# One layer of a hybrid decoder on one Trainium2 core: transposes given out inside the next product, query projections moved ahead

## The chip, the core and the metric

The kernel runs on one core of a Trainium2 chip. Six things work side by side on it: PE (the matrix engine, which also transposes by a product with the identity), DVE (the vector engine), ACT (the scalar engine, with tables for exponential, tanh and the like), POOL (the general engine), SP (here it only gives out transfers), and the DMA engines that carry them. Each engine takes its own instructions strictly in order and waits by semaphore for what another has to deliver. The metric is the device time of the whole program in microseconds (us); less is better.

## What is computed

One layer for 256 tokens of width 2048, in float32 accuracy, cut to what matters here:

```python
h = rmsnorm(x, pre_mix_norm)
z = h @ w_in                          # 2*1024 conv columns, 768 q latent, 512 kv latent, 64 rotary key
u = a * sigmoid(g)                    # GLU on the conv columns
u = silu(layernorm(causal_depthwise_conv(u, conv_w, conv_b)))     # 31 taps, over 1024 channels
q = rmsnorm(q_lat) @ w_uq             # 8 heads: 128 plain columns and 64 rotary ones each
kv = rmsnorm(kv_lat) @ w_ukv          # 8 heads: 128 key and 128 value columns each
q_pe, k_pe = apply_rope(q_pe), apply_rope(k_rope)      # one rotary key for all heads
attn = causal_attention(concat(q_nope, q_pe), concat(k_nope, k_pe), v)
mix = concat(rmsnorm(u), rmsnorm(attn)) @ w_out
x = x + rmsnorm(mix)
hf = rmsnorm(x)
x = x + rmsnorm((silu(hf @ w_gate) * (hf @ w_up)) @ w_down)       # inner width 5632
```

## The kernel before

**Products.** Every large product is made of three products of half-precision parts: a weight block is brought into a float32 stage buffer (four of them), ACT makes its high part (`whi`, L97) and DVE the rest (`wlo`, L98), in blocks of up to 2048 columns by 128 rows. For each row tile of a weight and each of the two token blocks of 128, PE then does high times high (L142), high times low (L143) and low times high (L144), for 512 columns at a time as a rule; two accumulators `acc` take the two token blocks. `mm3` is that loop; `mm3t` (L151 to L153) is the same the other way round, for 128 columns by 256 tokens, in an accumulator `tmp`.

**Stages.** (1) Four column blocks of the conv group. After each, ACT makes tanh and a scaled copy `av`, DVE makes `u` (L302), PE transposes it (L305) and ACT copies the result to `upad`. (2) Three blocks of 448 latent columns; ACT copies them out (L348), `latent_norm` scales the query latent and the kv latent (L330), splits them, and sends both through a transposing DMA. (3) The shared rotary key `kp`: eight small DVE operations a token block, the last L370, then a PE transpose L371; the rotary queries: one product of 36 matmuls, a copy `zq` (L381), six DVE operations a token block (L387 to L392), four transposes (L395). (4) The values, 48 matmuls. (5) Eight heads: `project` makes queries and keys of a head, two heads ahead; `scores` multiplies them (L447, L448), DVE takes the maximum (L453), ACT the exponential, POOL scales by the sum (L467); `attend` transposes the probabilities (L472 to L474), multiplies by the values, and POOL adds the squares (L486). (6) The attention rows of the output projection, four column blocks; between them the layer norm of the conv output: `ln_mean` (sum over channels L515, its mean over partitions L517, sum of squares after subtracting it L520), `ln_var` (L525, L531), swish, `conv_norm` (sums L538, L543). (7) The conv rows, then the feed-forward part, gate and up and down, which holds most of the products.

The depthwise convolution itself (31 taps for each of four channel groups, L275 and L283 on DVE, with some taps on ACT, L281) is given out in portions, `pump(n)`, between the other stages; the tuple `PUMPS` says how many taps after which.

**What sets the order.** The code is written in one sequence, and the scheduler that compiles it keeps an order for each engine that follows from that sequence and from a model of when inputs are there, so that a transposition written after a product may be placed some matmuls into the next. Transfers are all given out by SP's queue in one order; a stage buffer that is not free holds the queue behind it.

Of the kernel before, what the change touches and what calls it, by code (L numbers as in the profile page):

```python
# [17 lines left out]
P = 128  # L18
S = 256
# [22 lines left out]
# Exact power-of-two scales that centre the half-precision parts of an operand.  # L42
# [8 lines left out]
def hymba_layer(ctx: ExitStack, tc: tile.TileContext, x, xT, pos, inv_freq, g_pre, w_in, w_lat,  # L51
# [84 lines left out]
    def mm3(ps, x_of, wgt, tbs=(0, 1), k0=0, start=True, stop=True):  # L136
# [9 lines left out]
    def mm3t(ps, x_of, wgt, c0):  # L146
        """Feature-major product of 128 columns: ps += w[:, c0:c0+128].T @ x."""
# [43 lines left out]
    def rstd_of(ss, n, w=1, out_tile=None):  # L191
        """(ss / n + eps) ** -0.5"""
# [72 lines left out]
    def conv_tap(quarter, k):  # L265
        """One tap of a quarter of the channels, on the vector engine or shared with the scalar engine."""
# [22 lines left out]
    for j in range(4):  # L289
        if j == 0:  # L290
            ps = ps0
        else:
            wgt = wg1 if j == 1 else Weights(KD, 512).load(w_in[j], W_S)
            ps = [acc_tile(), acc_tile()]
            mm3(ps, h_of, wgt)
        for tb in range(NTB):
# [6 lines left out]
            tp = tmp_tile()  # L303
            for i in range(2):
                nc.tensor.transpose(tp[:, i * P : (i + 1) * P], u[:, i * P : (i + 1) * P], ident)  # L305
            nc.scalar.copy(upad[:, 2 * j : 2 * j + 2, PAD + tb * P : PAD + (tb + 1) * P],
                           tp[:, : 2 * P].rearrange("p (c t) -> p c t", c=2))
        conv_todo += [(j, k) for k in range(TAPS)]
        pump(PUMPS["conv"][j])

# [30 lines left out]
    # the columns are in the order query latent, kv latent, shared rotary key  # L341
    LN = (KL + QL + ROPE) // 3
    for j in range(3):
        wgt = Weights(KD, LN).load(w_lat[j], W_S)
        ps = [acc_tile()[:, :LN], acc_tile()[:, :LN]]
        mm3(ps, h_of, wgt)
# [10 lines left out]
    kpT = region(33, (S,))  # L357
    tp = tmp_tile()
    for tb in range(NTB):
        kp = work.tile([P, 2, ROPE], F32, tag="kp", name=nm("kp"))  # L360
        t1 = work.tile([P, ROPE], F32, tag="kt1", name=nm("kt1"))
        sin, cos = sincos[:, tb, 0, :], sincos[:, tb, 1, :]
        x1, x2 = z_kr[:, tb, 0:HALF], z_kr[:, tb, HALF:ROPE]
        nc.vector.tensor_tensor(t1[:, 0:HALF], x2, sin, op=ALU.mult)
        nc.vector.tensor_tensor(t1[:, HALF:ROPE], x1, sin, op=ALU.mult)
        nc.vector.tensor_tensor(x1, x1, cos, op=ALU.mult)
        nc.vector.tensor_tensor(x2, x2, cos, op=ALU.mult)
        nc.vector.tensor_tensor(kp[:, 0, 0:HALF], x1, t1[:, 0:HALF], op=ALU.subtract)
        nc.vector.tensor_tensor(kp[:, 0, HALF:ROPE], x2, t1[:, HALF:ROPE], op=ALU.add)
        nc.vector.tensor_copy(kp[:, 1, :], kp[:, 0, :])  # L370
        nc.tensor.transpose(tp[:, TB[tb]], kp.rearrange("p a b -> p (a b)"), ident)  # L371
    nc.scalar.copy(kpT, tp[:, :S])

# [1 line left out]
    qpT = region(8, (H // 2, S))  # L375
# [3 lines left out]
    for tb in range(NTB):  # L379
        zq = work.tile([P, H, ROPE], F32, tag="ss", name=nm("zq"), bufs=3)  # L380
        nc.scalar.activation(zq.rearrange("p h r -> p (h r)"), ps[tb], AF.Copy, scale=U)  # L381
# [11 lines left out]
        tp = tmp_tile()  # L393
        for i in range(H // 2):
            nc.tensor.transpose(tp[:, i * P : (i + 1) * P],  # L395
                                qp[:, 2 * i : 2 * i + 2, :].rearrange("p a b -> p (a b)"), ident)
        nc.scalar.copy(qpT[:, :, TB[tb]], tp.rearrange("p (i t) -> p i t", i=H // 2))
    pump(PUMPS["uqp"])

# [18 lines left out]
    proj = {}  # L418
    wq_cur = {}

    def project(h):
        if h % 2 == 0:
            wq_cur["q"] = Weights(QL // P, 256).load(w_uqn[h // 2], W_S)
            wq_cur["k"] = Weights(KL // P, 256).load(w_uk[h // 2], W_S)
        c0 = (h % 2) * P
        ps = tmp_tile()
        mm3t(ps[:, 0:S], lat_ft(qn), wq_cur["q"], c0)
        qT = work.tile([P, S], F32, tag="A", name=nm("qT"), bufs=3)
        nc.scalar.activation(qT, ps[:, 0:S], AF.Copy, scale=U)
        ps2 = tmp_tile()  # L430
        mm3t(ps2[:, 0:S], lat_ft(kvn), wq_cur["k"], c0)
        kT = work.tile([P, S], F32, tag="B", name=nm("kT"), bufs=3)
        nc.scalar.activation(kT, ps2[:, 0:S], AF.Copy, scale=U)
        proj[h] = (qT, kT)

    def scores(h):
        qT, kT = proj[h]
        o = ROPE * (h % 2)
        probs = []
# [73 lines left out]

    def ln_mean():
        nc.vector.tensor_reduce(csum, cacc.rearrange("p c t -> p t c"), axis=AX.X, op=ALU.add)  # L515
# [5 lines left out]

    def ln_var():
# [3 lines left out]
        rv = rstd_of(tp[:, 0:2], C, 2)  # L526
# [23 lines left out]
    mix = region(34, (NTB, D))  # L550
    for j in range(4):
        wgt = Weights(CB, 512).load(w_out[4 + j], W_S)
        ps = [acc_tile(), acc_tile()]
        mm3(ps, flat(mx_h[:, CB:], mx_l[:, CB:]), wgt)
# [145 lines left out]
def _tiles(w, cols):  # L700
    """Columns of w as [P, row tiles * columns]."""
# [74 lines left out]
```

## Time and profile of the kernel before

| what | value |
|---|---|
| median of 3 runs (lowest, highest) | 1021.36 us (1021.34, 1021.73) |
| profiled execution, span | 1019.8 us |
| PE busy | 988.7 us, 97% |
| DVE busy | 635.8 us, 62% |
| ACT busy | 502.6 us, 49% |
| POOL busy | 37.2 us, 4% |
| DMA, mean | 210 GB/s, 214.21 MB |

The profiled span is the time from the first to the last instruction that the profile sees on the core; the program's time, 1021.36, is 1.56 more. Shares are means over stages that are limited by different things. A row of a timeline gives the start, the duration (of pipelined matmuls it overlaps the next one's; the step from start to start is what one costs), and in brackets how long the engine was idle before it and which instruction ended that. The granted clock of PE, in the windows, is 1.00 at 2.4 GHz and 0.50 at 1.2 GHz.

### The profile page before, as it was taken

What the parts mean: (1) busy time and instruction counts of PE and PEld (TensorE: products, weight loads), DVE (VectorE), ACT (ScalarE), POOL (GpSimd) and SP (SyncE); (2) the same over time, 40 slices, a digit from 0 to 9 for tenths busy, and PEclk for the clock granted to TensorE, in tenths of its full rate; (3) what the DMA queues carried; (4) which work ended last, traced back from release to release, by engine and by line L of the source; (5) the groups of instructions that cost most, each with busy time, mean ns of one, the idle gap of its engine ahead of it and who ended that gap; (6) DMA issues with size and microseconds to landing.
All of it is one profiled execution on the core that took longest, in us unless ns stands there. A gap on an engine that the chain in (4) does not pass through costs nothing.

```text
span 1019.8 us, 11876 instructions
## 1 busy us (share of the span) xinstructions
PE 988.7 (97%) x4712; PEld 468.2 (46%) x4712; DVE 635.8 (62%) x724; ACT 502.6 (49%) x577; POOL 37.2 (4%) x50
## 2 busy tenths in 40 slices
PE   6999997999999999999999999999999999999996
PEld 2444553774444444444444444444444444444442
DVE  6699999999859874555555555554455444454412
ACT  7796665664747564444444444444444333343400
POOL 0000000034100100000000000000000000000000
PEclk9999998999999999999999999999999999999998
DMA  9874666577546978667666766677766665556302
GB/s 345 326 258 141 220 210 193 165 248 239 174 165 170 294 287 298 210 206 223 216 215 218 220 218 217 218 203 228 214 209 208 213 204 204 202 207 206 124 1 83
DMA packets 69512, 214.21 MB, mean 210 GB/s; under 512 B 41808, under 2 KB 42448, under 8 KB 47440
## 3 DMA queue, kind: packets, MB, share of 16 engines
q1 hardware_dynamic: 68736, 212.52, 63.6%
q8 instruction: 37, 0.61, 0.3%
q10 hardware_dynamic: 720, 0.93, 0.3%
q14 instruction: 19, 0.16, 0.0%
HBM read 202.16 MB, written 2.10 MB: 200 GB/s over the span
## 4 chain that ended last, share of the span: by engine, by line
PE 74%; DVE 11%; issue 4%; ACT 3%; POOL 2%; DMA 1%; DVEq 0%; POOLq 0%; ACTq 0%; SPq 0%
PE acc L144 23%; PE acc L143 23%; PE acc L142 23%; DVE wlo L98 3%; DVE arena L275 3%; ACT whi L97 1%; DVE arena L283 1%; POOL sm L196 1%; PE tmp L151 1%; PE tmp L152 1%; PE tmp L153 1%; POOL ss L467 1%; PE acc L448 1%; PE acc L447 1%; POOL arena L486 0%
## 5 line engine op out<-in xcount | busy, mean ns | idle before, releaser
L98 DVE SCALAR_TENSOR_TENSOR wlo<-st,whi 128x2048 f16<-128x2048 f32 (+4 forms) x191 | 419.7, 2200 | 281.6 <-ACT whi L97 281.6
L142 PE MATMUL acc<-whi,arena 128*128 128x512 f16 (+1 forms) x1436 | 543.9, 379 | 5.5 <-ACT whi L97 5.4
L143 PE MATMUL acc<-wlo,arena 128*128 128x512 f16 (+1 forms) x1436 | 544.0, 379 | 3.5 <-DVE wlo L98 3.4
L144 PE MATMUL acc<-whi,arena 128*128 128x512 f16 (+1 forms) x1436 | 543.5, 379 | 0.0
L97 ACT ACTIVATE whi<-st 128x2048 f16<-128x2048 f32 (+4 forms) x191 | 350.4, 1837 | 321.8 <-PE acc L144 291.0
L142 PEld LDWEIGHTS <-arena 128*128 128x128 f16 x1436 | 141.3, 98 | 172.0 <-ACT arena L102 4.9
L144 PEld LDWEIGHTS <-arena 128*128 128x128 f16 x1436 | 141.1, 98 | 170.7 <-issue 6.5
L143 PEld LDWEIGHTS <-arena 128*128 128x128 f16 x1436 | 140.9, 98 | 167.1 <-issue 3.1
L275 DVE SCALAR_TENSOR_TENSOR arena<-arena 128x256 f32<-128x256 f32 x184 | 78.0, 481 | 0.0
L621 ACT ACTIVATE sg<-acc,r_f 128x256 f32<-128x256 f32 x44 | 20.8, 475 | 58.4 <-PE acc L144 58.4
L623 DVE SCALAR_TENSOR_TENSOR a<-acc,r_f,sg 128x256 f32<-128x256 f32 x44 | 21.2, 483 | 20.6 <-ACT sg L621 20.6
L281 ACT ACTIVATE x_sb<-arena 128x256 f32<-128x256 f32 x56 | 25.4, 507 | 12.0 <-DVE arena L283 12.0
L652 ACT ACTIVATE junk<-acc 128x512 bf16<-128x512 f32 x8 | 4.8, 597 | 46.9 <-PE acc L144 46.8
L663 POOL TENSOR_TENSOR sm<-sm,neg_half 128x1 f32<-128x1 f32 x2 | 1.1, 540 | 663.3 <-DVE sm L661 663.3
L661 DVE TENSOR_SCALAR sm<-ssd,sm 128x1 f32<-128x1 f32 x2 | 0.4, 214 | 34.3 <-ACT junk L652 34.3
L151 PE MATMUL tmp<-arena,whi 128*128 128x256 f16 x80 | 21.8, 273 | 0.0
L153 PE MATMUL tmp<-arena,wlo 128*128 128x256 f16 x80 | 21.8, 273 | 0.0
L152 PE MATMUL tmp<-arena,whi 128*128 128x256 f16 x80 | 21.8, 273 | 0.0
L196 POOL TENSOR_TENSOR sm<-sm,neg_half 128x1 f32<-128x1 f32 (+1 forms) x12 | 11.9, 994 | 250.0 <-DVE sm L194 250.0
L98 DVE SCALAR_TENSOR_TENSOR ahl<-a,ahl 128x256 f16<-128x256 f32 x44 | 18.3, 417 | 2.5 <-ACT ahl L97 2.5
L97 ACT ACTIVATE ahl<-a 128x256 f16<-128x256 f32 x44 | 17.7, 406 | 3.9 <-DMA arena<-hl 3.9
L283 DVE TENSOR_TENSOR arena<-arena,x_sb 128x512 f32<-128x512 f32 x28 | 19.1, 681 | 0.1
(145 smaller groups left out, 329.4 us busy)
## 6 DMA issues: line engine op xcount, KB each, us to landing
st<-in_w_gu SPq DMA_DIRECT2D x88, 1024.0 KB, 5.1
st<-in_w_dn SPq DMA_DIRECT2D x44, 1024.0 KB, 4.8
st<-in_w_out SPq DMA_DIRECT2D x16, 1024.0 KB, 5.4
st<-in_w_in SPq DMA_DIRECT2D x14, 1024.0 KB, 9.3
st<-in_w_lat SPq DMA_DIRECT2D x12, 896.0 KB, 4.6
x_sb<-in_x SPq DMA_DIRECT2D x4, 1024.0 KB, 8.6
st<-in_w_uqn SPq DMA_DIRECT2D x4, 768.0 KB, 4.6
st<-in_w_uv SPq DMA_DIRECT2D x2, 1024.0 KB, 6.7
```

The lines of the kernel that those rows point to most:

```text
L97: nc.scalar.activation(hi, src, AF.Copy, scale=scale)
L98: nc.vector.scalar_tensor_tensor(lo, src, scale, hi, op0=ALU.mult, op1=ALU.subtract)
L142: nc.tensor.matmul(p_ap, xh, wh, start=(start and k == 0), stop=False)
L143: nc.tensor.matmul(p_ap, xh, wl, start=False, stop=False)
L144: nc.tensor.matmul(p_ap, xl, wh, start=False, stop=(stop and k == wgt.kt - 1))
L151: nc.tensor.matmul(ps, wh[:, c0 : c0 + P], xh, start=(k == 0), stop=False)
L152: nc.tensor.matmul(ps, wh[:, c0 : c0 + P], xl, start=False, stop=False)
L153: nc.tensor.matmul(ps, wl[:, c0 : c0 + P], xh, start=False, stop=(k == wgt.kt - 1))
L196: nc.gpsimd.tensor_tensor(r, t, neg_half.to_broadcast([P, w]), op=ALU.pow)
L275: nc.vector.scalar_tensor_tensor(cacc[:, cb, :], upad[:, cb, k : k + S], cw[:, cb, k : k + 1], cacc[:, cb, :], op0=ALU.mult, op1=ALU.add)
L281: nc.scalar.activation(t[:, i, :], upad[:, cb, k : k + S], AF.Copy, scale=cw[:, cb, k : k + 1])
L283: nc.vector.tensor_tensor(a, a, t, op=ALU.add)
```

## The change

It rearranges; no product is made smaller. Comments are dropped as well, which moves line numbers.

- At the start, nine products of 128x512 zeros go to PE, and ACT does one copy of a single column; before, the first product was PE's first work.
- `mm3` gets a table `at` of functions that are called ahead of a given row tile, six matmuls to a row tile. The GLU's two transposes for both token blocks are one function `turn`, called ahead of the fourth row tile of the next product.
- The rotary query product comes ahead of the rotary key's transposes; the query projections `project_q(0)` and `project_q(1)` (four heads) are put ahead of the transposes of the key and the queries, and kept in `qT_all`. `project_k` remains a head step of its own, and `scores` of a head are given out ahead of `attend` of the head before.
- The layer norm is cut in five steps: `ln_sum` after the first column block of the attention rows, `ln_mean` ahead of the fifth row tile of the second, `ln_var` and `ln_scale` ahead of the fourth and the seventh of the third, `conv_norm` ahead of the sixth of the fourth. Before, `ln_mean`, `ln_var` and `conv_norm` were written after the first, second and third block.

The diff, cut to its core:

```diff
+    def mm3(ps, x_of, wgt, tbs=(0, 1), k0=0, start=True, stop=True, at=None):
         for k in range(wgt.kt):
+            if at and k in at:
+                at[k]()
...
+    idle = region(20, (512,), F16)
+    nc.vector.memset(idle, 0.0)
+    nc.scalar.activation(idle[:, 0:1], idle[:, 0:1], AF.Copy)
+    warm = tmp_tile()
+    for i in range(9):
+        nc.tensor.matmul(warm, idle[:, 0:P], idle, start=True, stop=True)
...
+        def turn():
+            for tb, u in enumerate(us):
+                tp = tmp_tile()
+                for i in range(2):
+                    nc.tensor.transpose(tp[:, i * P : (i + 1) * P], u[:, i * P : (i + 1) * P], ident)
...
+        mm3(ps, h_of, wgt, at={3: turn})
+        turn = glu(j, ps)
...
+    turn_keys = rotary_key()
+    turn_q0 = rotary_query(0, ps[0])
+    project_q(0)
+    turn_keys()
+    turn_q0()
+    turn_q1 = rotary_query(1, ps[1])
+    project_q(1)
+    turn_q1()
...
-    project(0)
-    project(1)
+    project_k(0)
+    project_k(1)
+    held = {0: scores(0)}
     for h in range(H):
-        ss = scores(h)
+        if h in (0, 2):
+            project_q(2 + h // 2)
         if h + 2 < H:
-            project(h + 2)
+            project_k(h + 2)
+        if h + 1 < H:
+            held[h + 1] = scores(h + 1)
         pump(PUMPS["head"][h])
-        attend(h, ss)
+        attend(h, held.pop(h))
...
+    LN_AT = {1: {4: ln_mean}, 2: {3: ln_var, 6: ln_scale}, 3: {5: conv_norm}}
...
+        mm3(ps, flat(mx_h[:, CB:], mx_l[:, CB:]), wgt, at=LN_AT.get(j))
...
         if j == 0:
             pump(len(conv_todo))
-            ln_mean()
-        elif j == 1:
-            ln_var()
+            ln_sum()
         elif j == 2:
-            conv_norm()
```

What stands on the engines at three places, before and now. A name like `acc_535` is one buffer in use, `x2` a repeated instruction; weight loads between the matmuls are left out.

PE at the GLU transposes of the second column block, before (L305 is the transposition of `u`):

```order
L142 MATMUL acc_535<-whi_512,arena 128x512
...
L143 MATMUL acc_535<-wlo_513,arena 128x512
L305 MATMUL tmp_478<-ident,u_476 128x128 x2
...
L144 MATMUL acc_535<-whi_512,arena 128x512
...
L142 MATMUL acc_534<-whi_512,arena 128x512
L305 MATMUL tmp_488<-ident,u_486 128x128 x2
...
L143 MATMUL acc_534<-wlo_513,arena 128x512
```

The same place now (L314 is the transposition):

```order
L145 MATMUL acc_521<-whi_498,arena 128x512
...
L146 MATMUL acc_521<-wlo_499,arena 128x512
...
L147 MATMUL acc_521<-whi_498,arena 128x512
L314 MATMUL tmp_540<-ident,u_488 128x128 x2
L314 MATMUL tmp_544<-ident,u_494 128x128 x2
...
L145 MATMUL acc_520<-whi_498,arena 128x512
```

Before, the two token blocks' transposes came after 11 and after 13 matmuls of the next product; now both come after 18.

PE at the rotary key and queries, before (`kp` is the key of a token block, `qp` the queries, `acc_1386` and `acc_1387` the rotary query product, `acc_1469` and `acc_1470` the first values):

```order
L143 MATMUL acc_1386<-wlo_1377,arena 128x512
L371 MATMUL tmp_1352<-ident,kp_1353 128x128
...
L142 MATMUL acc_1386<-whi_1382,arena 128x512
L371 MATMUL tmp_1352<-ident,kp_1363 128x128
...
L144 MATMUL acc_1387<-whi_1382,arena 128x512
...
L142 MATMUL acc_1469<-whi_1465,arena 128x512
...
L142 MATMUL acc_1470<-whi_1465,arena 128x512
L395 MATMUL tmp_1434<-ident,qp_1426 128x128 x4
```

The same place now (`tmp_1448` to `tmp_1534` are query projections of heads 0 to 3):

```order
L147 MATMUL acc_1377<-whi_1372,arena 128x512
...
L154 MATMUL tmp_1448<-arena,whi_1444 128x256
...
L156 MATMUL tmp_1468<-arena,wlo_1445 128x256
L402 MATMUL tmp_1488<-ident,kp_1414 128x128
L402 MATMUL tmp_1488<-ident,kp_1423 128x128
L425 MATMUL tmp_1492<-ident,qp_1434 128x128 x4
...
L154 MATMUL tmp_1514<-arena,whi_1510 128x256
...
L156 MATMUL tmp_1534<-arena,wlo_1511 128x256
L425 MATMUL tmp_1554<-ident,qp_1500 128x128 x4
```

The key's first transpose stood after 14 of the 36 matmuls of the rotary query product; now all 36 and another 36 half-size ones of the query projections stand ahead of it. The first four query transposes stood 16 value matmuls behind that product; now they follow the key's transposes directly, with 36 half-size matmuls until the next four and the 48 of the values behind those.

DVE ahead of the first rotary query, before (`qp_1426`; L98 is a weight split, with the number of its columns):

```order
L370 COPY kp_1363<-kp_1363 128x64
L275 SCALAR_TENSOR_TENSOR arena<-arena 128x256 x4
L98 SCALAR_TENSOR_TENSOR wlo_1545<-st_1542,whi_1544 128x1024
L98 SCALAR_TENSOR_TENSOR wlo_1641<-st_1638,whi_1640 128x1536
L387 TENSOR_TENSOR qt_179_1427<-zq_1424,sincos 128x8x32
...
L392 TENSOR_TENSOR qp_1426<-qp_1426,qt_179_1427 128x8x32
```

The same place now:

```order
L396 COPY kp_1423<-kp_1423 128x64
L284 SCALAR_TENSOR_TENSOR arena<-arena 128x256
L348 SCALAR_TENSOR_TENSOR arena<-arena,sm_1358 128x512
L284 SCALAR_TENSOR_TENSOR arena<-arena 128x256
L98 SCALAR_TENSOR_TENSOR wlo_1606<-st_1603,whi_1605 128x2048
L98 SCALAR_TENSOR_TENSOR arena<-arena 128x512
L415 TENSOR_TENSOR qt_179_1435<-zq_1432,sincos 128x8x32
...
L420 TENSOR_TENSOR qp_1434<-qp_1434,qt_179_1435 128x8x32
```

Counting back to the splits of the rotary query's own weights, five splits (of 2048, 2048, 1536, 1024 and 1536 columns) stood ahead of the first query; now four do (1536, 1536, 2048, 2048). On ACT the copy of the last latent columns stood behind the splits of a key block of 1024 columns and a query block of 1536; now behind those of a value block of 2048 and a key block of 1024. On SP's queue this value block stands behind the two transposing transfers of the query latent, as the key block did before. On ACT the copies of kT for heads 4 and 5 stand behind a weight split, and the sum of the squares of the attention output is asked of PE after 34 matmuls of the first attention rows (before: 44).

## Rows read from the trace of the kernel before

**Rows 1.** The page, part 1: busy us, share of the span, instructions.

```profile
PE 988.7 (97%) x4712; PEld 468.2 (46%) x4712; DVE 635.8 (62%) x724; ACT 502.6 (49%) x577; POOL 37.2 (4%) x50
```

**Rows 2.** Windows: length; busy us (instructions) by engine; PE clock, DMA share, GB/s.

```profile
75.00:100.00 25.00, 23.75 (x113) 10.78 (x110) 25.00 (x44) 15.59 (x29) 0.00 (x0) 1.00 0.38 117
196.00:251.00 55.00, 51.27 (x308) 34.81 (x308) 50.51 (x105) 31.50 (x69) 22.25 (x23) 0.97 0.70 233
244.00:252.00 8.00, 7.54 (x30) 3.94 (x31) 6.63 (x16) 1.23 (x3) 2.00 (x3) 0.79 0.80 260
347.00:1011.00 664.00, 664.00 (x3079) 301.01 (x3077) 328.56 (x233) 272.89 (x226) 1.08 (x2) 1.00 0.64 204
```

**Rows 3.** PE's waits: instruction, releaser, us in total, times, longest.

```profile
PE tmp L371 <- DVE kp L370: 5.6, 1, 5.6
PE acc L142 <- ACT whi L97: 5.4, 1, 5.4
PE tmp L305 <- DVE u L302: 3.0, 3, 1.2
PE tmp L473 <- POOL ss L467: 2.3, 2, 2.0
PE acc L447 <- ACT kT L433: 1.1, 2, 1.0
PE tmp L543 <- DVE arena L538: 0.6, 1, 0.6
PE tmp L531 <- DVE dg L530: 0.6, 1, 0.6
PE tmp L525 <- DVE arena L520: 0.3, 1, 0.3
```

**Rows 4.** Timeline of PE, rotary stretch: start, us, operation [idle before <-releaser].

```profile
156.76 0.38 PE L143 MATMUL acc<-wlo,arena 128*128 128x512 f16 x1
...
162.97 0.63 PE L144 MATMUL acc<-whi,arena 128*128 128x512 f16 x1
...
167.23 0.56 PE L142 MATMUL acc<-whi,arena 128*128 128x512 f16 x1
...
181.35 0.27 PE L151 MATMUL tmp<-arena,whi 128*128 128x256 f16 x1
181.46 0.27 PE L152 MATMUL tmp<-arena,whi 128*128 128x256 f16 x1
```

**Rows 5.** Timeline of ACT: the first table load.

```profile
3.07 1.28 ACT L102 ACT_TABLE_LOAD   x1 [3.07 <-DMA arena<-in_xT]
```

**Rows 6.** Timeline of PE, first product: waits for weight parts.

```profile
12.19 0.38 PE L143 MATMUL acc<-wlo,arena 128*128 128x512 f16 x1 [0.88 <-DVE wlo L98]
...
21.79 0.38 PE L143 MATMUL acc<-wlo,arena 128*128 128x512 f16 x1 [1.46 <-DVE wlo L98]
```

**Rows 7.** Timeline of DVE: the GLU of the second column block.

```profile
56.11 0.42 DVE L302 SCALAR_TENSOR_TENSOR u<-th,av 128x256 f32<-128x256 f32 x1 [1.19 <-ACT av L300]
```

**Rows 8.** Timeline of DVE: end of the first rotary query, and a split.

```profile
171.98 0.42 DVE L392 TENSOR_TENSOR qp<-qp,qt 128x256 f32<-128x256 f32 x1
172.31 1.22 DVE L98 SCALAR_TENSOR_TENSOR wlo<-st,whi 128x1024 f16<-128x1024 f32 x1
```

**Rows 9.** Timeline of POOL: the last head's scaling of its probabilities.

```profile
241.11 3.30 POOL L467 TENSOR_SCALAR ss<-ss,sm 128x128 f32<-128x128 f32 x2
```

**Rows 10.** Timeline of DVE: the column sums of the layer norm.

```profile
250.88 3.73 DVE L515 TENSOR_REDUCE arena<-arena 128x256 f32<-128x2048 f32 x1
```

**Rows 11.** Timeline of PE: the layer norm's mean.

```profile
256.10 0.59 PE L517 MATMUL tmp<-arena,ones_c 128*128 128x256 f32 x2
```

**Rows 12.** DMA issues: queue, operation, count, KB each, us to landing.

```profile
st<-in_w_in SPq DMA_DIRECT2D x14, 1024.0 KB, 9.3
...
st<-in_w_uqn SPq DMA_DIRECT2D x4, 768.0 KB, 4.6
st<-in_w_uv SPq DMA_DIRECT2D x2, 1024.0 KB, 6.7
```

More of the change, by code (lines that the diff above doesn't have):

```diff
@@ L134, in load @@
             return self
-    def mm3(ps, x_of, wgt, tbs=(0, 1), k0=0, start=True, stop=True):
+    def mm3(ps, x_of, wgt, tbs=(0, 1), k0=0, start=True, stop=True, at=None):
         for k in range(wgt.kt):
+            if at and k in at:
+                at[k]()
             wh, wl = wgt.parts[k]
@@ L287, in pump, with glu @@
             conv_tap(*conv_todo.pop(0))
[L289 to L295, printed above, removed]
+    def glu(j, ps):
+        us = []
         for tb in range(NTB):
@@ L302, in hymba_layer @@
             nc.vector.scalar_tensor_tensor(u, th, 1.0, av, op0=ALU.add, op1=ALU.mult)
[L303 to L309, printed above, removed]
+            us.append(u)
+        def turn():
[3 more added lines that the diff above has]
+                    nc.tensor.transpose(tp[:, i * P : (i + 1) * P], u[:, i * P : (i + 1) * P], ident)
+                nc.scalar.copy(upad[:, 2 * j : 2 * j + 2, PAD + tb * P : PAD + (tb + 1) * P],
+                               tp[:, : 2 * P].rearrange("p (c t) -> p c t", c=2))
+            conv_todo.extend((j, k) for k in range(TAPS))
+            pump(PUMPS["conv"][j])
+        return turn
+    turn = glu(0, ps0)
+    for j in range(1, 4):
+        wgt = wg1 if j == 1 else Weights(KD, 512).load(w_in[j], W_S)
+        ps = [acc_tile(), acc_tile()]
+        mm3(ps, h_of, wgt, at={3: turn})
+        turn = glu(j, ps)
     z_all = region(16, (NTB, KL + QL + ROPE))
@@ L345, in hymba_layer @@
         ps = [acc_tile()[:, :LN], acc_tile()[:, :LN]]
-        mm3(ps, h_of, wgt)
+        mm3(ps, h_of, wgt, at={3: turn} if j == 0 else None)
         for tb in range(NTB):
@@ L354, in hymba_layer @@
     latent_norm(z_kv, g_kv, KL, kv_hl, kvn)
+    qpT = region(8, (H // 2, S))
     kpT = region(33, (S,))
[L358 to L375, printed above, removed]
+    qT_all = region(16, (H, S))
     wgt = Weights(QL // P, 512).load(w_uqp, W_S)
@@ L378, in hymba_layer, with rotary_key, turn_keys, rotary_query @@
     mm3(ps, lat_of(qn), wgt)
-    for tb in range(NTB):
+    def rotary_key():
+        kps = []
+        for tb in range(NTB):
+            kp = work.tile([P, 2, ROPE], F32, tag="kp", name=nm("kp"))
+            t1 = work.tile([P, ROPE], F32, tag="kt1", name=nm("kt1"))
+            sin, cos = sincos[:, tb, 0, :], sincos[:, tb, 1, :]
+            x1, x2 = z_kr[:, tb, 0:HALF], z_kr[:, tb, HALF:ROPE]
+            nc.vector.tensor_tensor(t1[:, 0:HALF], x2, sin, op=ALU.mult)
+            nc.vector.tensor_tensor(t1[:, HALF:ROPE], x1, sin, op=ALU.mult)
+            nc.vector.tensor_tensor(x1, x1, cos, op=ALU.mult)
+            nc.vector.tensor_tensor(x2, x2, cos, op=ALU.mult)
+            nc.vector.tensor_tensor(kp[:, 0, 0:HALF], x1, t1[:, 0:HALF], op=ALU.subtract)
+            nc.vector.tensor_tensor(kp[:, 0, HALF:ROPE], x2, t1[:, HALF:ROPE], op=ALU.add)
+            nc.vector.tensor_copy(kp[:, 1, :], kp[:, 0, :])
+            kps.append(kp)
+        def turn_keys():
+            tp = tmp_tile()
+            for tb in range(NTB):
+                nc.tensor.transpose(tp[:, TB[tb]], kps[tb].rearrange("p a b -> p (a b)"), ident)
+            nc.scalar.copy(kpT, tp[:, :S])
+        return turn_keys
+    def rotary_query(tb, ps_tb):
         zq = work.tile([P, H, ROPE], F32, tag="ss", name=nm("zq"), bufs=3)
-        nc.scalar.activation(zq.rearrange("p h r -> p (h r)"), ps[tb], AF.Copy, scale=U)
+        nc.scalar.activation(zq.rearrange("p h r -> p (h r)"), ps_tb, AF.Copy, scale=U)
         qp = work.tile([P, H, ROPE], F32, tag="ss", name=nm("qp"), bufs=3)
@@ L392, in hymba_layer, with turn_queries, project_q, project_k @@
         nc.vector.tensor_tensor(qp[:, :, HALF:ROPE], qp[:, :, HALF:ROPE], t1[:, :, HALF:ROPE], op=ALU.add)
[L393 to L397, printed above, removed]
+        def turn_queries():
+            tp = tmp_tile()
+            for i in range(H // 2):
+                nc.tensor.transpose(tp[:, i * P : (i + 1) * P],
+                                    qp[:, 2 * i : 2 * i + 2, :].rearrange("p a b -> p (a b)"), ident)
+            nc.scalar.copy(qpT[:, :, TB[tb]], tp.rearrange("p (i t) -> p i t", i=H // 2))
+        return turn_queries
+    kT_of = {}
+    wk_cur = {}
+    def project_q(i):
+        wgt = Weights(QL // P, 256).load(w_uqn[i], W_S)
+        for h in (2 * i, 2 * i + 1):
+            ps = tmp_tile()
+            mm3t(ps[:, 0:S], lat_ft(qn), wgt, (h % 2) * P)
+            nc.scalar.activation(qT_all[:, h, :], ps[:, 0:S], AF.Copy, scale=U)
+    def project_k(h):
+        if h % 2 == 0:
+            wk_cur["k"] = Weights(KL // P, 256).load(w_uk[h // 2], W_S)
+        ps = tmp_tile()
+        mm3t(ps[:, 0:S], lat_ft(kvn), wk_cur["k"], (h % 2) * P)
+        kT = work.tile([P, S], F32, tag="B", name=nm("kT"), bufs=3)
+        nc.scalar.activation(kT, ps[:, 0:S], AF.Copy, scale=U)
+        kT_of[h] = kT
+    turn_keys = rotary_key()
[6 more added lines that the diff above has]
+    turn_q1()
     pump(PUMPS["uqp"])
@@ L416, in hymba_layer @@
     nc.vector.tensor_scalar(gat, gat, O_S, None, op0=ALU.mult)
[L418 to L434, printed above, removed]
     def scores(h):
-        qT, kT = proj[h]
+        qT, kT = qT_all[:, h, :], kT_of[h]
         o = ROPE * (h % 2)
-        probs = []
         mxs = smalls(2)
@@ L512, in hymba_layer, with ln_sum @@
     g8 = const.tile([P, CB], F32, name="g8")
+    def ln_sum():
+        nc.vector.tensor_reduce(csum, cacc.rearrange("p c t -> p t c"), axis=AX.X, op=ALU.add)
     def ln_mean():
-        nc.vector.tensor_reduce(csum, cacc.rearrange("p c t -> p t c"), axis=AX.X, op=ALU.add)
         mu = tmp_tile()
@@ L520, in ln_mean @@
         nc.vector.tensor_reduce(csum2, csq.rearrange("p c t -> p t c"), axis=AX.X, op=ALU.add)
+    rvs = []
     def ln_var():
@@ L525, in ln_var, with ln_scale @@
             nc.tensor.matmul(tp[:, tb : tb + 1], csum2[:, TB[tb]], ones, start=True, stop=True)
-        rv = rstd_of(tp[:, 0:2], C, 2)
+        rvs.append(rstd_of(tp[:, 0:2], C, 2))
+    def ln_scale():
+        rv = rvs[0]
         dg = work.tile([P, NTB, P], F32, tag="A", name=nm("dg"), bufs=3)
```

1 line of the change is left out of this document (removed).

## The prediction

> **What bounds the kernel now.** I read the page's first line of engines: the reader is to see that PE, the matrix engine, is busy 988.7 us of a span of 1019.8, and that nothing else comes near [rows 1]. So about 31 us can be won at all, and only where PE stands still or runs at the lower clock. The windows say where that can be: from 347 to 1011 us PE is busy 664.00 of 664.00 with 3079 matmuls, 0.2157 us each, so nothing that the change does can shorten that part; it can only move it to an earlier start [rows 2]. The list of PE's waits then gives the candidates by name [rows 3]: the rotary key L371 5.6 us once, the first weights L142 5.4, the GLU transposes L305 3.0 in three, the last head's transposes L473 2.3, the scores L447 1.1, three layer-norm steps 1.6 together. The change goes at all of them except the first weights' arrival. The other thing to see is VectorE (DVE). It is busy 25.00 of 25.00 us from 75 to 100, and it stays so nearly all the way to the column sums of the layer norm (50.51 of 55 from 196 to 251) [rows 2]. A wait of PE on DVE in that stretch is then not a matter of PE's order only: putting the transpose later lets PE work meanwhile, but the value comes no sooner, because DVE has its queue to get through.
>
> **The change part by part** (each in us of the profiled span; minus is a gain).
>
> *Products on zeros.* They add nine 128x512 matmuls ahead of the first product. At the lower clock one takes 0.426 (first to last of the rows at 162.97 and 167.23, ten steps in 4.26 [rows 4]), so 3.8 us. They need ACT's table load (1.28 us [rows 5]), which no longer waits for the transfer of x, and end about 6.5 if they start behind it near 2.7 (earlier than its 3.07, since nothing is waited for), where the first real matmul waited until 5.4 [rows 3]. The real ones then go at full rate, but PE reaches the weight parts at 12.19 and 21.79 and waits for them anyway (0.88 and 1.46 [rows 6]): the first product lasts as long as its transfers. Cost 0. Bounds: +2 if the zeros end late and the waits for weights do not cover it, −2.5 (12 matmuls at 0.426 instead of 0.216) if the time came back whole.
> The Trainium skill, page "TensorE: Matmul & The Clock Gate", section "Why this matters for your kernels", has it that matmuls ahead of those that count keep these off the lower rate; this would make the start 2.5 faster. The trace has no such run to compare; its waits for the weights speak against it.
>
> *GLU transposes.* Before, PE came to them after 11 to 13 matmuls of the next product and waited 3.0 in three, 1.2 the longest [rows 3]. Now they stand after 18, both token blocks together. 18 matmuls are 3.9 us, and 5 more than 13 are 1.1, about the longest of these waits. DVE also gets an extra weight split in front of u, filling its own gap of 1.19 at 56.11 [rows 7]: that is a gain for DVE which counts below. In the last block the second u comes late for a 448-wide product, about 0.6 of wait. −3.0 + 0.6 = −2.4. Bounds −3.0 and 0.
>
> *Rotary key and queries.* Before: a wait of 5.6 [rows 3] and then 11 matmuls (162.97 to 167.23) at 0.426 instead of 0.216, 2.3 us: 7.9 lost [rows 2, 4]. After: the same place is reached at 156.76 + 0.38 − 2.4 = 154.7. The rotary-query product has 22 matmuls left there (14 were done), 22 × 0.216 = 4.8, and the 36 of project_q(0) at 0.109 each are 3.9 [rows 4]: PE stands at L402 at 163.4. Both keys come before the queries in DVE's order, so whatever L402 waits lies within what comes next. But the four transposes L425 that follow need all of qp of block 0, the last operation of which, L392, runs at 171.98 for 0.42 and so ends at 172.40 [rows 8]. Ahead of it DVE now has one 1024-column weight split less (7168 columns of splits where 8192 stood), about 1.1 us by the row of one at 172.31 (1.22) [rows 8], and it is some 0.8 ahead from the filled GLU gap: 172.4 − 1.1 − 0.8 = 170.5. PE waits from 163.6 to 170.5, 6.9 us, and, as it did after the 5.6, I take it to fall to the lower clock for some 11 matmuls' worth, 2.3: 9.2 lost. The wait has moved from the key to the query, net +1.3. Nothing else is put in front of L425 that PE could do. The second L425 follows 36 matmuls later (PE not before 177, qp of block 1 about 175.5): no wait. Bounds: −7.9 if DVE got to qp some 7 earlier (nothing in its queue would allow that), +5.8 if the transfers of the rival below come late (1.3 + 4.5).
>
> *Heads.* Waits before: L447 1.1, L473 2.3, together 3.4 [rows 3]; behind the 2.0 of the last head the clock is 0.79 on the mean from 244 to 252 [rows 2], 8 × 0.21 = 1.7, less what fell in the wait itself: 1.5. So 4.9 could go. In the new order scores are given a head ahead, which hides the softmax of each head behind the next. But the copies of kT for heads 4 and 5 still stand behind a weight split on ACT that waits for PE (one such wait was 1.0 [rows 3]), some 5 us more of DVE's work stands in front of the score maxima of the first three heads, POOL's scaling of the last head (3.30 for its two [rows 9]) still stands behind the addition of squares, and the sum of squares of the outputs is asked for after 34 matmuls instead of 44. Each priced by its nearest row: head 1 softmax 1.1, kT4 1.0, kT5 0.8, last head 2.0 with 1.5 of clock, sum 0.9: 7.3 in all if each bites. Bounds −4.9 (all hidden) and +2.4 (all bite). What is waited for has not moved, so I stand nearer the upper end, three quarters of the way: +0.5.
>
> *Layer norm.* The waits of 0.32, 0.61 and 0.63 [rows 3] are each moved behind more matmuls of the next product: L531's step from 30 matmuls to 36, L525's from 17 to 18, L543's from 2 to 20 of the conv rows. They go: −1.6. What is late next: the mean, moved to 24 matmuls instead of some 27. Its matmul at 256.10 did not wait, and csum ended at 250.88 + 3.73 = 254.6 [rows 10, 11], so there is about 1.5 − 0.65 = 0.85 of slack, and DVE being 1 ahead covers the gains forecast so far (0.6). Bounds −1.6 and 0.
>
> Sum: 0 − 2.4 + 1.3 + 0.5 − 1.6 = −2.2, a span of 1017.6. The median of the runs shown, 1021.36, lies 1.56 above the profiled span, so 1021.36 − 2.2 = **1019.2**.
>
> **The rivals.**
> *A. All head waits go.* Speaking for it: scores a head ahead leave the work of a whole further head for maximum, exponential and scaling. Against: the queues of ACT and POOL named above. Then −4.9 instead of +0.5, but not in full: DVE's csum limits how early the layer norm can start, to 0.85 of slack, 1.2 of the filled GLU gap and about half of the 4.5 us that DVE idles between 196 and 251, so −4.2 up to there, and −1.6: 1021.4 − 5.8 = 1015.6.
> *B. The clock at the start counts.* If PE's rate and not the transfers set the length of the first product, its 12 matmuls at the lower rate give back 12 × 0.21 = 2.5: 1016.7. Against it stand the two waits for weights inside that product [rows 6]. The rule of the Trainium skill named above leads here.
> *C. The gains are eaten.* The heads stand at their upper end: −2.4 + 1.3 + 2.4 − 1.6 = −0.3, so 1021.1. For it: each of the instructions waited for is still queued behind the same kind of work. Against: all five would have to bite.
> *D. Slower: the latent columns are copied out late.* In ACT's new order the copy of the last latent columns stands behind two weight splits, the second half of the value weights and the first key weights, whose transfers are queued behind the two transposing transfers of the query latent. Before, smaller blocks stood there. The norm of the kv latent and so qp hang on that copy. The largest that stood there, a uqn block, landed 4.6 us after its issue, the value weights 6.7. Should their 1 MB land as slowly as the w_in rows, 9.3, qp is up to 9.3 − 4.6 = 4.7 later [rows 12], nearly all of it PE's wait: 1019.2 + 4.5 = 1023.7. It decides the sign from 4.2 us on. For it: DMA is loaded in that stretch; against: these rows' slow landings are from the start of the kernel, where all queues were full.
> That the change does not do what it says is no rival: the orders show every step in its new place; only its worth is open.
>
> **How the numbers follow.** About 0.2% (2.0 us) is what a measurement of this kernel can tell from no change: faster is under 1019.3, slower over 1023.4. My forecast 0.45, with an own range of 1017.0 to 1021.3, half of it on either side of 1019.3; A 0.22, B 0.05, C 0.13, D 0.15. Faster: 0.45 × 0.52 + 0.22 + 0.05 = 0.50; same 0.45 × 0.48 + 0.13 = 0.35; slower 0.15. The range takes in A's 1015.6 with a little below and stops short of D's full price: 1014.8 to 1023.0.
>
> **What would show it right or wrong.** In the list of waits after: the key's 5.6 gone, and in its place a wait of L425 on DVE qp of 6 to 8 us, with the lower clock behind it; under 3 us there and my rotary step is wrong, over 10 and D is right. L305's successors under 1 us in sum. In the heads the waits on kT and the last head's scaling stay, 4 to 7 us in all; if they sum under 2, A is right. In the layer norm no wait over 0.3 on its four steps, or one on csum if A holds. The first window: still waits for wlo near 12 and 22 us, and from 22 us on the same instants as before; an earlier product there speaks for B. The gapless stretch of 664 us keeps its length; if that changes, the whole reckoning is wrong.

## The result and the profile after

The changed kernel takes 1027.27 us (1026.23 to 1029.26, 4 runs) where the kernel before takes 1021.55: ratio 1.0057, interval 1.0042 to 1.0073. It is slower, where 1019.2 was forecast and 1014.8 to 1023.0 given as the range. The profiled run after took 1026.23, span 1024.5: it is the fastest of its four, so its 4.7 us over the span of 1019.8 are a little less than the 5.7 between the medians.

The waits of PE in the changed kernel, the list that answers to [rows 3] (its wait for the zeros and those for weight parts left out):

```profile
PE tmp L425 <- DVE gat L477: 6.6, 1, 6.6
...
PE acc L489 <- ACT kT L448: 2.9, 4, 0.9
...
PE tmp L514 <- POOL ss L509: 2.6, 2, 2.0
PE tmp L596 <- DVE arena L591: 2.1, 1, 2.1
PE tmp L548 <- POOL arena L528: 2.1, 1, 2.1
...
PE tmp L402 <- DVE kp L396: 0.9, 1, 0.9
PE tmp L314 <- DVE u L307: 0.3, 1, 0.3
```

The GLU's 3.0 has become 0.3, the key's 5.6 has become 0.9 and then 6.6 for the query; `gat`, the instruction named there, only follows the query's last one on DVE (start 170.09, 0.42 long). The waits for kT have grown from two (1.1) to four (2.9), that for the conv norm's sums from 0.6 to 2.1; the 2.1 for POOL's sum of squares is new. The list alone does not say where the time went, since some waits hide others. For that I compare when PE starts the same matmul of the large products in the two traces (the n-th matmul of `mm3`; after minus before, us; 7.85 taken off at the end of the values, for the 72 half-size matmuls at 0.109 that were moved there from the heads):

| at the end of | after − before | this stage | forecast |
|---|---|---|---|
| first product | +0.20 | +0.2 | 0 |
| latent columns | −3.10 | −3.3 | −2.4 |
| values | −1.85 | +1.25 | +1.3 |
| first block of attention rows | +3.15 | **+5.0** | +0.5 |
| third block | +1.74 | −1.4 | −0.9 |
| first half of the conv rows | +4.88 | **+3.1** | −0.6 |
| the last product | +4.89 | 0 | 0 |

The windows show the clock behind a wait of 2.0 (226.89) and one of 2.1 (292.08), and the unchanged part (columns as in [rows 2]):

```profile
226.00:234.00 8.00, 6.99 (x31) 5.05 (x31) 3.72 (x16) 3.38 (x9) 2.76 (x5) 0.79 0.40 133
290.00:298.00 8.00, 5.92 (x23) 2.66 (x23) 6.44 (x5) 2.94 (x2) 0.69 (x1) 0.79 0.44 152
351.00:1015.00 664.00, 664.00 (x3078) 300.70 (x3077) 329.48 (x234) 273.26 (x226) 1.08 (x2) 1.00 0.63 204
```

664 us stay 664, as in [rows 2]. All is decided before 312 us.

**Where the heads lose.** From the last value matmul to the end of the first block of attention rows PE waits 8.3 us, before 3.7; the lower clock costs 1.7 in both. The waits are 2.9 for kT (before 1.1), 2.9 for POOL's scaling (2.3), 2.1 for its sum of squares (none) and 0.3 for a copy on ACT. POOL's timeline in the changed kernel, and DVE's beside it:

```profile
223.13 0.76 POOL L528 TENSOR_TENSOR arena<-arena,sq 128x256 f32<-128x256 f32 x1 [3.44 <-ACT sq L524]
223.88 3.41 POOL L509 TENSOR_SCALAR ss<-ss,sm 128x128 f32<-128x128 f32 x2
...
237.69 0.83 POOL L509 TENSOR_SCALAR ss<-ss,sm 128x128 f32<-128x128 f32 x2 [3.61 <-DVE sm L505]
238.57 0.72 POOL L528 TENSOR_TENSOR arena<-arena,sq 128x256 f32<-128x256 f32 x1
...
247.19 2.48 POOL L528 TENSOR_TENSOR arena<-arena,sq 128x256 f32<-128x256 f32 x1 [3.29 <-ACT sq L524]
```

```profile
224.39 2.29 DVE L98 SCALAR_TENSOR_TENSOR wlo<-st,whi 128x2048 f16<-128x2048 f32 x1
...
246.80 2.29 DVE L98 SCALAR_TENSOR_TENSOR wlo<-st,whi 128x2048 f16<-128x2048 f32 x1 [0.72 <-ACT whi L97]
```

The same two scalings take 0.83 at 237.69 and 3.41 at 223.88, the same addition 0.72 and 2.48; both slow ones meet a weight split on DVE and end about 0.6 after it ends. So it is with POOL's operations of both kernels between 190 and 250 us: those in both traces that last over 1.5 us (four before, four after) each overlap a split by 1.0 to 2.3 us, and the rest, under 1.0 each, by 0.4 at most. Before, one such meeting was on PE's path, the scaling of [rows 9] that makes the 2.0 of [rows 3]. Now two are, 2.01 at 226.89 and 2.07 at 249.72, and behind the slow addition of 241.17 (1.58) the scaling comes late, 0.9 of wait. e1, e4 and e13, which have the same order of the heads, show the same waits: it is the order that decides which operations meet a split. The Trainium skill, page "SBUF — State Buffer", section "SBUF: two separate sides", says that DVE and GpSimd have a pair of ports in common that one of them holds for a whole instruction; the durations here agree, but no run shows the ports themselves.

**Where the conv norm loses.**

```profile
292.08 0.58 PE L596 MATMUL tmp<-ones,arena 128*128 128x1 f32 x4 [2.08 <-DVE arena L591]
```

ACT's table load ahead of the swish, before and now:

```profile
269.08 1.28 ACT L534 ACT_TABLE_LOAD   x1
...
277.87 1.28 ACT L587 ACT_TABLE_LOAD   x1
```

The chain to these sums is a product with the scale on DVE, a table load, eight swish and eight split operations and a square on ACT, and a sum on DVE. Before it began at 269.02 (L531) and ended at 284.86; now it begins at 272.13: L584 stands 6 matmuls later, PE was already 1.7 late, and ACT does two copies, a weight split and the table load (274.72 to 279.16) where before it had the table load behind it by 270.4 and could start the swish at 272.06. The swish now starts at 279.16, 7.1 later: 3.1 from L584's start, 4.0 from what lies between. The sums are there at 291.9, 7 us later than before, and PE comes to them 5.6 later. Behind the wait the next 8 full-size matmuls or so run at the lower level, 0.43 each from 293.54: 1.7 lost.

### The profile page after: what moved, and what is told of

It reads as the page before. It is cut to its first block, busy times and chain, and to the rows that moved or that the text cites. A ratio compares the mean times of both kernels' runs of the same rounds, so it can differ in the third digit from the quotient of the medians.

```text
span 1024.5 us, 11893 instructions
## 1 busy us (share of the span) xinstructions
PE 990.7 (97%) x4721; PEld 470.1 (46%) x4721; DVE 635.9 (62%) x725; ACT 502.8 (49%) x578; POOL 33.3 (3%) x50
## 4 chain that ended last, share of the span: by engine, by line
PE 70%; DVE 14%; ACT 4%; issue 3%; POOL 1%; DMA 1%; DVEq 0%; POOLq 0%; ACTq 0%
PE acc L147 23%; PE acc L146 23%; PE acc L145 23%; DVE wlo L98 5%; DVE arena L284 5%; ACT whi L97 2%; DVE arena L292 1%; DMA st<-in_w_uqn 1%; POOL sm L205 1%; DMA st<-in_w_out 1%; POOL ss L509 0%; PE tmp L520 0%; DVE x_sb L649 0%; POOL arena L528 0%; ACT arena L587 0%
## 5 line engine op out<-in xcount | busy, mean ns | idle before, releaser
L98 DVE SCALAR_TENSOR_TENSOR wlo<-st,whi 128x2048 f16<-128x2048 f32 (+4 forms) x191 | 419.8, 2200 | 289.3 <-ACT whi L97 289.3
L98 DVE SCALAR_TENSOR_TENSOR ahl<-a,ahl 128x256 f16<-128x256 f32 x44 | 18.3, 417 | 2.5 <-ACT ahl L97 2.5
```

Source lines behind the costliest of these rows:

```text
L98: nc.vector.scalar_tensor_tensor(lo, src, scale, hi, op0=ALU.mult, op1=ALU.subtract)
```

## The experiments

Medians are to be read against the kernel before, measured beside each (1021.3 to 1021.6). Stages are read from one profiled run each, and runs of one order differ above all by what the lower clock takes: the changed kernel, e1 and e13 have the same heads and lose 5.0, 8.0 and 7.5 there, with 1.7, 5.1 and 3.4 us taken by the lower clock (1.7 in the kernel before).

**One part at a time.** e1 leaves out the nine products; e2, e3 and e4 put one part into the kernel before: the GLU's `turn`, the layer norm's `LN_AT`, or the rotary part with the heads.

```diff
-    for i in range(9):
-        nc.tensor.matmul(warm, idle[:, 0:P], idle, start=True, stop=True)
```

> The changed kernel without the nine products on zeros; everything else of the change stays. Theory (the first product lasts as long as its transfers): in the changed kernel the first product ended 0.20 us later than before, so the time falls by 0.2, to about 1027.0 from 1027.3, and PE waits for weight parts near 12 and 22 us again. Rival (the zeros' time comes back through the full clock): without them it is up to 2.5 slower, about 1029.7.

1026.34, 1.0048 (1.0031 to 1.0065): the same as with them within the intervals. The zeros neither gain nor cost. The matmuls behind them go at 0.216 a step from 6.51 on, where without them the first ones take 0.426, but the first product ends no sooner: 31.70 with the zeros, 31.75 in e1, 31.50 before. So the 0.2 is not theirs, though the expectation took it for theirs.

> The kernel before with the GLU transposes moved (18 matmuls into the next product), nothing else. Theory (DVE sets when the rotary key is there): PE is 3.1 us ahead at the end of the latent columns, as in the changed kernel, but the key comes only about 1 earlier, so the wait for it grows from 5.6 to about 7.5 and the time falls by 0.8 to 1.2, to about 1020.5. Rival (PE carries the gain through): 3.1 faster, 1018.4.

1025.44, 1.0042 (1.0027 to 1.0057): neither theory. PE is 3.35 ahead at the end of the latent columns, 1.64 at the end of the values (it waits 1.5 for the query latent's transfer and 5.6 for the key), 0.8 behind at the attention rows and 3.75 at the end:

```profile
PE tmp L383 <- DVE kp L382: 5.6, 1, 5.6
...
PE tmp L514 <- POOL arena L498: 2.4, 1, 2.4
PE tmp L555 <- DVE arena L550: 2.1, 1, 2.1
PE acc L459 <- ACT kT L445: 2.0, 2, 1.8
PE acc L145 <- DMA arena<-arena: 1.5, 1, 1.5
```

The heads and the layer norm are not changed in that kernel, yet they show waits on POOL and on the conv norm's sums like those of the whole change, only from other offsets; of the 3.3 lost in the heads 1.7 is the lower clock.

> The kernel before with the layer norm's steps moved into the products, nothing else. Theory (the step after the variance is now later, ACT does a weight split, two copies and its table load ahead of the swish, and the sums of the conv norm are asked for too early): three waits of 1.4 go, one of 2.1 with 1.75 of lower clock comes in place of 0.6, so +1.8, about 1023.3, with a wait on the sum over channels of about 2. Rival (that wait in the changed kernel came from what the heads had delayed): the waits go and it is 1.5 faster, 1020.0.

1022.91, 1.0015 (1.0005 to 1.0024), with a wait of 2.07 on the sums: the theory's direction and wait; in the landmarks −0.8 on the three steps and +3.1 on the sums.

> The kernel before with the query projections ahead of the rotary transposes and scores a head ahead, nothing else. Theory (the new order of the heads itself makes five waits, on ACT's copies of kT and on POOL): the rotary part about -0.7 to +1, the heads +5, so about +4.5, 1026.0. Rival (the heads wait only because the GLU's gain makes PE come early to a DVE that is behind): +0.5 to +2, 1022 to 1023.5.

1029.75, 1.0086 (1.0071 to 1.0101): more than both. Values −0.8 (7.04 less 7.85), heads +4.8, as the theory has it; then +4.7 in a layer norm that is not changed. The heads do not need the GLU's gain to be slow. The 4.7 was in neither theory.

**POOL.** e5 (the changed kernel) and e6 (the one before) give POOL's jobs to ACT and DVE:

```diff
-            nc.gpsimd.tensor_scalar(d, d, rc[:, qb : qb + 1], 0.0, op0=ALU.mult, op1=ALU.add)
+            nc.scalar.activation(d, d, AF.Copy, scale=rc[:, qb : qb + 1])
...
-            nc.gpsimd.tensor_tensor(sq_sum, sq_sum, sq, op=ALU.add)
+            nc.vector.tensor_tensor(sq_sum, sq_sum, sq, op=ALU.add)
```

> The changed kernel with POOL's two jobs in the heads given to others: the scaling of the probabilities to ACT (two operations a head), the sum of squares to DVE (one a head). Theory (a POOL operation that meets a weight split of DVE is held until the split ends, and PE waits for it): the waits of 2.01, 0.63, 0.29 and 2.07 go, and the lower clock behind the first (1.7), so about 6 faster, less 1 to 3 for ACT and DVE: 1022 to 1024. Rival (the heads are late on the whole, because DVE and ACT have too much ahead of them): these waits come back as waits on ACT and DVE, and the time stays within 1 of 1027 or grows.

> The kernel before with the same two jobs taken from POOL. Theory: the waits of 2.01 and 0.29 and the lower clock behind them (1.5) go, 3.8 less, 1017.8; part of it may be lost to ACT and DVE, so 1018 to 1020. Rival (late on the whole): no change or slower, 1021 to 1023.

e5: 1023.85, 1.0026 (1.0016 to 1.0037), 3.4 less, the theory's number; the waits on POOL are gone, but those on kT grow from 2.9 to 4.8, as the rival has it, and the heads are shorter by 2.6. e6: 1021.32, 0.9995 (0.9985 to 1.0004), no gain at the end, the rival's number; but PE is 4.9 ahead after the first attention block, and hands it back: 1.5 ahead of the conv rows, 3.1 in them, with 2.1 of wait at the sums.

So POOL cost the heads of the kernel before even more (5.2) than those of the changed one (2.6), and is not what makes the new order slower. Without POOL, the heads of the changed kernel (e5) and of the kernel before (e6; columns as in [rows 2]):

```profile
187.52:250.76 63.24, 57.49 (x342) 39.35 (x341) 57.87 (x136) 42.26 (x95) 0.70 (x1) 0.97 0.54 178
181.44:244.95 63.51, 62.30 (x409) 44.88 (x408) 61.22 (x143) 47.38 (x104) 0.00 (x0) 1.00 0.58 199
```

The changed kernel does 72 matmuls (7.85 us) less in this stage and takes as long; PE waits 5.8 us there against 1.2. It is the same in e9 and e14 against e10 and e15 (63.3 to 63.6 in all four). The query projections were work that PE did while DVE and ACT prepared the heads, and the change took them out.

**The order of the heads.** e7 takes the lead of the scores out of the changed kernel, e8 puts it into the one before.

> The changed kernel with the loop over the heads as it was (scores of a head directly ahead of its own probabilities), the query projections staying ahead of the rotary transposes. Theory (with the query projections gone from the loop, PE has too little left to cover the copies and the softmax): each head then shows most of its softmax, 2 to 3 us more a head, 8 to 20 slower than the changed kernel, 1035 to 1047. Rival (giving scores out a head ahead is itself what costs): faster than the changed kernel by 3 to 5, 1022 to 1024.

> The kernel before with scores given out a head ahead, nothing else; query projections stay in the loop. Theory (the filler matters): the waits on kT and on the last head's scaling shrink, 1 to 3 faster, 1018.5 to 1020.5. Rival (scores ahead cost by themselves): 3 to 5 slower, 1024.5 to 1026.5.

e7: 1036.35, the theory's number: the lead is needed once the query projections are gone from the loop. But of the 10.8 that its heads are longer than the changed kernel's, 8.5 is the lower clock and only 2.4 wait. e8: 1026.38, 1.005 (1.0035 to 1.0065): the rival's number, but not its reason. Of the 4.2 that its profiled run is behind, 1.4 arise ahead of the heads (the key's wait is 6.6 there), 0.7 up to the end of the first attention block and 2.1 in the layer norm. In the heads it trades the wait of 2.0 on POOL's scaling for one of 1.6 at 225.42, with the lower clock behind it (0.76 from 225 to 230). Set beside e4 it shows what the projections are worth there: with the lead alone the heads lose 0.7 and PE waits 3.9, with the projections taken out as well they lose 4.8 and PE waits 7.9 (lower clock 1.7 in both).

**The sums later.** The conv norm's sums are asked of PE in the second block of the conv rows; that block's results and the first's are copied out behind it. In e9, e10 and e12 the sums' input lay where the gain of the post norm is loaded, so that the conv rows are scaled by another number there, and in e9 and e10 PE waited for that load; in e13 to e17 it has its own place.

```diff
-    LN_AT = {1: {4: ln_mean}, 2: {3: ln_var, 6: ln_scale}, 3: {5: conv_norm}}
+    LN_AT = {1: {4: ln_mean}, 2: {3: ln_var, 6: ln_scale}}
...
+    mm3(early[1:], mxc_of, wo[1], (0,), at={4: conv_norm})
```

> The changed kernel with POOL's two jobs in the heads given to ACT and DVE, and the conv norm's sums asked of PE in the second block of the conv rows (ahead of its fifth row tile, the first block's result being copied out behind it) instead of in the fourth block of the attention rows. Theory (the wait of 2.1 on these sums and the lower clock behind it are all that was lost there): 3.1 less than with POOL's jobs moved alone (1023.85), 1020.7. Rival (the sums are late for the conv rows' results anyway, so the wait only moves): within 0.7 of 1023.85.

> The kernel before with POOL's two jobs in the heads given to ACT and DVE, and the conv norm's sums asked of PE in the second block of the conv rows. Theory (the 4.6 us won in the heads were given back at the layer norm, by 2.1 of wait and about 1 of lower clock at these sums and 1.4 one step earlier): 3.1 less than with POOL's jobs moved alone (1021.3), 1018.2, faster than both kernels. Rival (the layer norm's chain on DVE and ACT sets the end of the conv rows whatever PE does): 1021.3.

1022.97 (1.0015, 1.0003 to 1.0027) and 1019.76 (0.9984, 0.9975 to 0.9994): 0.9 and 1.6 less where 3.1 was expected, with 2.3 and 2.0 of wait on that load in place of the wait on the sums.

> The changed kernel with the conv norm's sums asked of PE in the second block of the conv rows, and their input kept in a place that no later load takes (in the two runs before it was overwritten by the gain vector, and PE waited 2.0 to 2.3 for that load). Theory (the wait of 2.1 and the lower clock behind it): PE enters the conv rows as before and leaves them 3 earlier, 1027.3 - 3.1 to 3.8, 1023.5 to 1024.2. Rival (the chain on ACT and DVE behind these sums ends too late for any place): 1026.5 to 1027.5.

> The changed kernel with both: POOL's jobs in the heads given to ACT and DVE, the conv norm's sums later with their own place. Theory: 1023.85 - 3.1 = 1020.7, the two terms that were mis-sized both taken away. Rival: 1023.9.

> The kernel before with POOL's jobs in the heads given to ACT and DVE, and the conv norm's sums later with their own place. Theory (what was won in the heads, 4.6, is no longer given back at these sums): 1021.3 - 3.1 = 1018.2 or, from the run with the overwritten place, 1019.8 - 2.0 = 1017.8. Rival: 1019.8 or more.

e13: 1023.50, 1.0021 (1.0006 to 1.0036); e14: 1020.20, 0.9989 (0.998 to 0.9998); e15: 1017.23, 0.9956 (0.9943 to 0.9968). Each where the theory put it, within 1 us. The conv norm's sums cost the changed kernel 3.8, POOL 3.3 to 3.4, and with both away it is 1.1 faster than the kernel before. On the kernel before the same two edits give 4.1. Like with like, the changed kernel is still 3.0 behind with both away (e14 against e15, 1018.72 to 1022.27 against 1016.47 to 1017.33), where it was 5.7 behind with neither: the two places are about half of the loss. In the traces of these two the heads are where it is behind, by 7.7 (waits 4.4 against 1.2, lower clock 3.4 against none).

**The rotary wait.** e11 puts the value products ahead of the query transposes, e12 adds the other two edits.

```diff
     turn_keys()
-    turn_q0()
-    turn_q1 = rotary_query(1, ps[1])
     project_q(1)
-    turn_q1()
...
+        if j == 0:
+            turn_q0()
+            turn_q1 = rotary_query(1, psq[1])
+        else:
+            turn_q1()
```

> The changed kernel with the second pair of query projections and the first value product put ahead of the rotary query transposes of block 0, and the second value product ahead of those of block 1. Theory (the 6.55 us in front of those transposes are DVE's, and what follows is DVE's and ACT's too): the wait goes, PE is some 8 ahead at the end of the values, and most of it comes back as waits on kT, POOL and DVE in the heads and at the mean: 0 to 3 faster than the changed kernel, 1024 to 1027. Rival (PE is the bound from there on): 8.8 faster, 1018.5.

> The changed kernel with all three edits: POOL's jobs in the heads given to ACT and DVE, the conv norm's sums later, the value products ahead of the rotary query transposes. Theory: 3.4 less for POOL and 3.1 for the sums as before, and from the rotary part 0 to 3, so 1018 to 1021. Rival (PE is the bound from the rotary part on): 1012.

e11: 1027.28, no gain. e12: 1026.54, where the theory had 1018 to 1021: 3.6 slower than e9, which lacks only the moved products; the values end sooner, and the heads are 6.0 longer, 2.6 of it wait and 3.4 lower clock. In e11 PE ends the values 5.9 earlier than in the changed kernel, and then waits for kT, whose copy is behind on ACT, and runs 190 to 195 at the lower level:

```profile
182.92 0.63 PE L425 MATMUL tmp<-ident,qp 128*128 128x128 f32 x4 [1.27 <-DVE qp L420]
...
189.48 0.80 PE L492 MATMUL acc<-kT,arena 128*128 128x128 f32 x2 [3.31 <-ACT kT L448]
```

```profile
190.00:195.00 5.00, 5.00 (x17) 2.75 (x16) 3.91 (x11) 1.74 (x3) 0.00 (x0) 0.50 0.34 74
```

Taking a wait of 6.6 away from PE won nothing.

**Putting it together.** e16 is e15 with the changed kernel's other layer-norm steps, e17 is e16 with the GLU transposes.

> The same with the changed kernel's other layer-norm steps too (mean, variance and scale given out inside the products). Theory: three waits of 1.4, 0.2 and 0.2 go as well, 1 to 1.8 less, 1016 to 1017. Rival (the later scale makes the swish, and so the first results of the conv rows, late): no gain or up to 1 slower, 1018 to 1019.

> The kernel before with POOL's jobs in the heads given to ACT and DVE, the layer norm moved with the sums later, and now the GLU transposes moved as well. Theory (PE's gain ahead of a stage that DVE sets is given back there): PE is 2 to 3 ahead at the end of the latent columns, the wait for the rotary key or in the heads grows by about as much, and the time is within 1 of the 1016.6 without it. Rival (with the two held-up places gone the gain arrives): 1013.5 to 1014.5.

e16: 1016.57, 0.9953 (0.9941 to 0.9966), the fastest, 4.8 under the kernel before; against e15 the intervals overlap. e17: 1018.84, 0.9964 (0.9951 to 0.9978), 2.3 over e16 where the theory allowed 1 (the runs of the two overlap): the GLU's gain is there at the end of the latent columns (−3.2) and is lost by the third attention block, where it is 2.7 behind e16. Its longest new waits are 2.5 for the layer norm's second sums and 1.8 for kT.

## Why the prediction was wrong

- *Zeros*: right, 0: with and without them the first product ends within 0.05 (e1), so B is out.
- *GLU*: the term was right where it was counted, −3.3 against −2.4. What was wrong is that it was carried to the end. The text itself said that a gain of PE in a stretch that DVE sets brings the value no sooner, but the sum added the gain all the same. Alone it ends in a loss of 3.9 (e2), and with the two other costs away still in no gain (e17).
- *Rotary*: right in place and size. The query's last operation was forecast to end at 170.5 and ended there (170.51). PE waited 0.9 and 6.6, together 7.5, where 6.9 was forecast; that the net still is +1.25 against +1.3 is partly luck, as 0.7 was gained in this stage outside the waits, which no term names.
- *Heads*: the step that failed first. "What is waited for has not moved, so I stand nearer the upper end" gave +0.5 between bounds of −4.9 and +2.4; +5.0 came. What had moved is the work that covered the waits: 7.85 us of query projections left the heads, and the sum has no term for it. The runs show +0.7 for the lead alone (e8) and +4.8 with the projections out (e4), PE's waits 3.9 and 7.9. The places were right and the prices too low: all that could bite was put at 7.3, and 10.0 came, kT 2.9 for 1.8, POOL's scaling 2.9 for 2.0, the sum of squares 2.1 for 0.9, the clock 1.7 for 1.5; only the softmax, 0.3 for 1.1, was less. The sign named for this step, 4 to 7 us on kT and the scaling, held all the same (5.8) and so could not tell. POOL's slow operations, which [rows 9] shows, were taken for a property of the last head; they are meetings with a DVE split, but they cost the old order as much (e6). (By its own figures three quarters of the way is +0.6.)
- *Layer norm*: the first two waits went as forecast (0.9; the stage gained 1.4). The step that failed is "L543's from 2 to 20 of the conv rows. They go": it counted the 18 matmuls gained on PE's side, and not what the change does to the chain between, where L584 itself moved and ACT's table load fell behind a split and two copies. +3.1 instead of −0.6, of which 1.7 is the lower clock behind a wait of 2.1; e13 shows 3.8.
- *Rivals*: none held. C named the heads, with too small a price. D asked for a late copy of the latent columns, and the rotary part was on time. The slower case was priced in the wrong stage. The 31 us named as the most to be won leave out the lower clock, under which PE counts as busy.

Left open: what sets the 63 us of the heads once POOL is out of them (DVE is busy 57.9 of 63.2 in e5, and PE waits mostly for kT from ACT), when the clock falls, and why stages that an edit does not touch shift by 1 to 2 us (the key in e8, the layer norm in e2, e4 and e8). In e2 ACT's split ends at 272.6, ahead of the table load, where before it ended at 269.1; that fits, but no run moved that split alone.

## What to carry to other kernels

A wait moved off one engine is a gain only as far as the engines behind it are ahead: find the next place where another engine's work must be complete, and cap the gain by the slack there. Work that an engine does while others prepare its next input is a cover: when a change moves it out, price the stage that it leaves as well. When a change shifts the start of a chain over several engines, price the chain's own order on each of them, not only the room that the waiting engine was given. And look for operations in the trace whose duration varies: what stretches them is a term of its own, and in these kernels giving POOL's small operations to ACT and DVE and asking for the sums one block later was worth 4.1 us without any of the reordering.

## What the runs showed of the hardware

POOL's addition of 128x256 took 0.72 us alone and 2.48 beside a 2048-column split on DVE. A wait of PE of 2.0 to 2.1 us was followed by the lower clock in some places (0.43 a matmul behind 292.08) and not in others (behind 249.72 the window 250 to 260 shows 1.00), and the same wait of 2.08 at the conv norm's sums not in e1 (290 to 300 at 1.00), so that it cost 2 or nearly 4.
